# Binding the copies of the weight sums behind the projection's stores, and the residual's scaling into VectorE's operations

## The chip, the cores and the metric

The kernel runs on one core of a Trainium2 chip. A core has TensorE (PE, matrix products; PEld is its loading of weights), VectorE (DVE), ScalarE (ACT) and GpSimd (POOL), each with its own in-order queue of instructions, and 16 DMA engines. Transfers are issued here from two queues: SyncE's (SP), which does nothing else, and POOL's. On each queue a transfer that has to wait for a semaphore holds up everything written behind it. The metric is device time in microseconds (us); lower is better. The profile is one execution, with its own time.

## What is computed

One decoder layer on x of 2048 tokens by 1024 channels (float32), with a conditioning vector c that gives six rows of shift, scale and gate:

```
mod = silu(c) @ w_ada + b_ada            -> sh1, sc1, g1, sh2, sc2, g2
h   = x * (1 + sc1) + sh1
z   = h @ w_in                           -> gate_b, gate_c, v_conv, v_pool (512 columns each)
mix = [gate_b * conv3(gate_c * v_conv), pool(v_pool) @ w_pool * pool_scale] @ w_out
x   = LayerNorm(ALPHA * x + (1 + g1) * mix) * ln1_g + ln1_b        ALPHA = 2 ** 0.25
h   = x * (1 + sc2) + sh2
f   = relu(h @ w_mlp_in) ** 2 @ w_mlp_out                          hidden width 4096
out = LayerNorm(ALPHA * x + (1 + g2) * f) * ln2_g + ln2_b
```

`pool` is a causal mean over windows of 2, 4, 8 and 16 tokens minus the token.

## The kernel before

**Precision.** Every float32 operand is split into a high and a low part (`split`, L81 on ScalarE and L82 on VectorE), and each product is three matmuls (`mm3`, L86 to L88): high by high, high by low, low by high.

**Batches and stages.** The tokens are worked in two batches of T = 1024 (`b` = 0 and 1). Each goes through the input projection (four groups `j` of columns, with convolution and pooling behind each group), the output projection (`out_proj`), the MLP up (`up`, eight groups of 512 hidden columns) and the MLP down (`down`). The projection of batch 0 (`in_proj_0`) begins with `first_group`, which works through the eight slices of the contraction as they land: two rows of `w_ada`, a slice of `w_in` and a tile of x for each, loaded on SP one behind another (`in_turn`, L101), with the matmuls of L403. The other large products, batch 1's projection (`in_proj_1`) among them, use seven products of blocks in place of eight (`seven`); they need sums of blocks of the weights and of the activations, which are made by VectorE or kept in DRAM.

**The weight sums of the change.** Batch 1's `down` takes one part of its work a level further (the "fine" units, matmuls of L1164): blocks of a quarter's width, with sums of quarters of `w2`. These sums are made without any engine: `sum_quarters` (L997, L1000) issues transfers from DRAM to DRAM on POOL's queue. For each of three sets `n` and two halves, step 0 copies four blocks of 512 KB into `wquart` (eight transfers a set), and steps 1, 2 and 3 add onto them with accumulating transfers (four, two and two a set): 48 transfers in all, 24 copies and 24 accumulations. Sets 0 and 1 read weights that are inputs (`w2q`), set 2 reads sums that batch 0's MLP stores (`w2sum`). In the program they are written in batch 1's projection, behind each group `j`, as `SUM_TURNS` has it, and for the last steps in batch 1's `out_proj`:

```
SUM_TURNS = (((0, 0),), ((1, 0), (0, 1)), ((2, 0), (1, 1), (0, 2)), ((2, 1), (1, 2), (0, 3)))   # (set, step) by group
```

**The stores beside them.** Behind each of the groups 0 to 2 of a projection, `store_mixed` (L342, L344) stores the group's outputs and their sums to `msum`, four transfers on POOL; the output projection loads them on SP. The rows of x that `out_proj` adds come by `load_x` (L860) on POOL, into o buffers; VectorE adds the products to them out of PSUM (L877, L884).

**The residual.** `residual(b)` makes ALPHA times the normalised rows: it loads the two rows ln1_g and ln1_b, broadcast over the partitions (`row`, L211, on SP), scales both by ALPHA on ScalarE (L1105, L1106), then for each of eight tiles loads the normalised tile from `nsave` (L1109; on POOL in batch 1, on SP in batch 0), multiplies and adds on VectorE (L91) and stores to `rsave` (L1112). It is a generator: `down` starts it at one unit of its work (`next(later)`), which issues the row loads, and resumes it at four later ones (`later.send(done)`), each of which does two tiles. `done` is the pair of the last instructions of a weight split, ScalarE's and VectorE's.

**The order.** A planner makes the order on each engine's queue: of the instructions whose inputs and buffers its own estimate takes for ready it issues the one that stands first in the program, so an instruction without inputs may come far ahead of its place. `tc.issue_after(i)` orders what its block issues on i's engine behind i, and binds nothing on other engines. Buffers are shared by tag: 28 of `h`, 12 of `o`, 6 of `w`, 5 of `r`, 8 PSUM banks.

Of the kernel before, what the change touches and what calls it, by code (L numbers as in the profile page):

```python
# [11 lines left out]
ALU = mybir.AluOpType  # L12
# [5 lines left out]
H = 512  # L18
# [8 lines left out]
ALPHA = 2.0 ** 0.25  # L27
# [16 lines left out]
def tile_hybrid_layer(ctx: ExitStack, tc: tile.TileContext, opening, xT, x, wada, vec, win0, win,  # L44
                      wins, wpool, wout, wmix, w1, w2, w2q, rows, out):
    nc = tc.nc
# [18 lines left out]
    def t_o(w=T, dt=F32):  # L65
        return mk(big, [P, w], dt, "o", 12)
# [23 lines left out]
    def tt(out_, a, b_, op):  # L90
        return nc.vector.tensor_tensor(out_, a, b_, op=op)  # L91
# [84 lines left out]
    msum = tc.dram_tile([7, NG - 1, P, H], F32, name="msum")  # L176
# [154 lines left out]
    def mixed_sums(y, pt, u, v):  # L331
        a11, a21, a12, a22 = y[:, :H], y[:, H:], pt[:, :H], pt[:, H:]
        s1, s2, s4 = u[:, :H], u[:, H:T], v[:, :H]
        tt(s1, a21, a22, ALU.add)
        tt(s2, s1, a11, ALU.subtract)
        tt(a21, a11, a21, ALU.subtract)
        tt(s4, a12, s2, ALU.subtract)
        return a21, s1, s2, s4

    def store_mixed(j, y, pt, u, v):  # L340
        for i, r in ((0, y), (2, pt), (4, u[:, :T])):
            nc.gpsimd.dma_start(msum[i : i + 2, j].rearrange("a p n -> p a n"),  # L342
                                r.rearrange("p (a n) -> p a n", a=2))
        nc.gpsimd.dma_start(msum[6, j], v[:, :H])  # L344


    def first_group(A):
# [268 lines left out]
    def in_proj_1(X, W, first_w):  # L616
        mixed = []
        ops = Operands(mixed)

        def cut(rows_, h):  # L620
            return [r[:, o + h * H : o + h * H + H] for r, o in rows_]

        def keep(dst, banks):
            for p in range(2):
                nc.scalar.copy(dst[p], banks[p])

        def add(dst, banks):
            for p in range(2):
                tt(dst[p], dst[p], banks[p], ALU.add)

        def group(j):
            x_, y_, z_ = {}, {}, {}
            ready = W if j == 0 else block_weights(wins[j])
            product = seven(ready, X, None if j else first_w)
            v, u = t_o(WW), t_o(WW)
            values = (v, HALO), (u, 2)
            product(0, x_, True)
            keep(cut(values, 0), x_)
            nc.vector.tensor_copy(v[:, :HALO], vhalo[:, j, :])
            nc.vector.tensor_copy(u[:, :2], uhalo[:, j, :])  # L640
            if j == 0:
                inputs(X, ORDER[3][1])
            product(1, y_, True)
            add(cut(values, 0), y_)
            if j == 0:
                inputs(X, ORDER[4][1])
            yield
            gc, gb = t_o(), t_o()
            gates = (gc, 0), (gb, 0)
            last = j == NG - 1  # L650
            product(2, x_, False)
            keep(cut(values, 1), x_)
            if j == 0:
                inputs(X, ORDER[5][1])
            product(3, z_, True)
            keep(cut(gates, 1), z_)
            if j == 0:
                inputs(X, ORDER[6][1])
            if last:
                ops.begin(0)  # L660
            yield
            product(4, x_, False)
            add(cut(gates, 1), x_)
            if last:
                ops.begin(1)
            product(5, z_, False)
            add(cut(values, 1), z_)
            if last:
                ops.weights(0, 1)
                pt = pool_mid(1, j, v)  # L670
            product(6, x_, False)
            keep(cut(gates, 0), x_)
            if last:
                ops.weights(1, 1)
                ops.second(0)
            yield
            if not last:
                pt = pool_mid(1, j, v)
            y = gc
            for hs in halves if last else [slice(0, T)]:  # L680
                w = hs.stop - hs.start
                tt(u[:, 2 + hs.start : 2 + hs.stop], u[:, 2 + hs.start : 2 + hs.stop], gc[:, hs], ALU.mult)
                conv(j, u[:, hs.start : hs.stop + 2], y[:, hs], w)
                tt(y[:, hs], y[:, hs], gb[:, hs], ALU.mult)
                if last and hs.start == 0:
                    mixed.extend([y[:, :H], None, pt[:, :H], pt[:, H:]])
                    ops.third(0)
                    ops.third(1)
            sums = mixed_sums(y, pt, u, v)
            if last:  # L690
                mixed[1] = sums[0]
                mixed.extend(sums[1:])
            else:
                store_mixed(j, y, pt, u, v)
            for n, step in SUM_TURNS[j]:
                sum_quarters(n, step)

        groups = [group(j) for j in range(NG)]
        for _ in range(3):
            next(groups[0])  # L700

        for j in range(1, NG):
            last = j == NG - 1
            next(groups[j])
            if not last:
                next(groups[j])
            next(groups[j - 1], None)
            if last:
                next(groups[j])
            next(groups[j])  # L710
        next(groups[-1], None)
        return ops


    SUM_TURNS = (((0, 0),), ((1, 0), (0, 1)), ((2, 0), (1, 1), (0, 2)), ((2, 1), (1, 2), (0, 3)))
# [276 lines left out]
    def sum_quarters(n, step):  # L992
        for hf in range(2):
            for i, what in SUM_STEPS[step]:
                src = quarter_sum(n, hf, int(what)) if what in ("0", "1") else weight_quarter(n, what, hf)
                if step:
                    nc.gpsimd.dma_start(quarter_sum(n, hf, i), src, accum_op=ALU.add,  # L997
                                        max_dma_last_dim=4096)
                else:
                    nc.gpsimd.dma_start(quarter_sum(n, hf, i), src)  # L1000
# [100 lines left out]
    def residual(b):  # L1101
        ag, ab = row(t_o(D), rows[0]), row(t_o(D), rows[1])
        after = yield
        with tc.issue_after(after[0]):
            nc.scalar.mul(ag, ag, ALPHA)  # L1105
        nc.scalar.mul(ab, ab, ALPHA)  # L1106
        for t in range(8):
            r = t_o(D) if b else t_r()
            (nc.gpsimd if b else nc.sync).dma_start(r, nsave[t])  # L1109
            tt(r, r, ag, ALU.mult)  # L1110
            tt(r, r, ab, ALU.add)
            nc.gpsimd.dma_start(rsave[t], r)  # L1112
            if t % 2:
                yield


    def down(b, F, g2, close):
# [158 lines left out]
        for n, (kind, i, part_) in enumerate(units):  # L1276
            while ahead_ < len(units) and (
                    ahead_ <= n + 1 or b and held + size[units[ahead_][0]] <= 28):
                made.append(operands(*units[ahead_]))
                held += size[units[ahead_][0]]  # L1280
                ahead_ += 1
            ops, done = made.pop(0)
            if made and made[-1][1]:
                done = made[-1][1]
            if kind == "f":
                fine_product(i, part_, ops)
                if (i, part_) == (1, 6):
                    for t in range(4):
                        add(t, lo_, X[t])
                if (i, part_) == (3, 6):  # L1290
                    for t in range(4):
                        tt(F[t][:, hi_], F[t][:, hi_], F[t + 4][:, hi_], ALU.add)
            else:
                if b == 0 and n < 2:
                    ada(G2 + 4 * n, G2 + 4 * n + 4, nc.sync.dma_start, lambda: t_o(D))
                if b == 0 and 2 <= n < 6:
                    sum_x(n - 2, done)
                if n == (0 if b else 5):
                    next(later)
                if kind == "c" and i == 0 and part_ in (1, 2, 4, 6) or b == 0 and 5 <= n < 9:  # L1300
                    later.send(done)
                if kind == "h" and i in (4, 6) and part_ == 1:
                    rest[i] = saved(hi_ if i == 4 else lo_)
                    if i == 6:
                        close.turn()
                banks, new, then = table[i]
                whole = kind == "h"
                matmuls(banks, ops, new, part_ == 0, part_ == (1 if whole else NC - 1), then,
                        part_ == 1 and i in (4, 5, 6) if whole else False)
            held -= size[kind]  # L1310
            if b == 0 and n == 4:
                row_of(g2, mod[:, G2 : G2 + KD])
# [177 lines left out]
```

## Time and profile before

| | |
|---|---|
| median of 3 runs | 1828.07 us (1827.97 to 1833.69) |
| profiled execution, its own time | 1825.45 us |
| its span | 1823.6 us |
| mean granted clock of TensorE | 0.977 |
| TensorE busy | 1741.1 us, 95% |
| VectorE, ScalarE, GpSimd busy | 1329.2, 894.0, 276.2 us |
| moved by DMA | 514.04 MB, 282 GB/s in the mean |

The span runs from the first to the last instruction on the chip; the time of the execution holds a little more. Busy time of TensorE is the sum of overlapping matmuls cut to the clock, so a stretch without a gap reads as wholly busy. The granted clock is the share of full speed that TensorE was given. In the views, "x8" counts instructions, a bracket says how long the engine stood idle before and what released it, "SPq" and "POOLq" are the queues, q1 the transfers of SP and q0 those of POOL.

### The profile page before, as it was taken

The numbers are of one execution on the slowest core, as the hardware profiler recorded it, in microseconds if no ns is written. First come the engines' busy times: TensorE is split into PE (matmuls) and PEld (weight loads), VectorE is DVE, ScalarE is ACT, GpSimd is POOL, SyncE is SP. The second block draws the span as 40 slices with busy tenths as digits, with TensorE's granted clock in tenths as the row PEclk, the third lists the DMA queues.
The fourth block names the chain that finished last, engine by engine and source line by source line (L and its number), as shares of the span: only waits on it lengthen the run. The fifth ranks groups of instructions, "written<-read, shape, count | busy, mean of one in ns | idle before, by whom it ended". The sixth has DMA issues, their size and how long they took to land.

```text
span 1823.6 us, 22633 instructions
## 1 busy us (share of the span) xinstructions
PE 1741.1 (95%) x8132; PEld 1455.6 (80%) x8132; DVE 1329.2 (73%) x1756; ACT 894.0 (49%) x1206; POOL 276.2 (15%) x493
## 2 busy tenths in 40 slices
PE   4599999999988999999999999999999999999998
PEld 3488888888876887888887888888888887999986
DVE  2289869887748649676868778878766667997675
ACT  1242335855434545453557334585545455676552
POOL 3112222112323310000100001011222112000000
PEclk6799999999998999999999999999999999999999
DMA  9999986777898899988876227576455449999884
GB/s 316 269 384 354 349 312 219 283 265 294 334 289 331 325 337 417 390 298 301 321 284 231 88 99 280 173 250 222 169 211 205 168 176 380 419 407 325 309 311 182
DMA packets 158304, 514.04 MB, mean 282 GB/s; under 512 B 18288, under 2 KB 23920, under 8 KB 157936
## 3 DMA queue, kind: packets, MB, share of 16 engines
q1 hardware_dynamic: 102960, 315.97, 47.5%
q0 software_dynamic: 55232, 196.64, 30.4%
q8 instruction: 63, 1.03, 0.2%
q14 instruction: 49, 0.40, 0.1%
HBM read 359.97 MB, written 177.73 MB: 295 GB/s over the span
## 4 chain that ended last, share of the span: by engine, by line
PE 79%; DMA 12%; DVE 3%; issue 3%; ACT 2%; POOL 1%; SPq 0%; DVEq 0%; POOLq 0%; ACTq 0%
PE ps L87 24%; PE ps L88 24%; PE ps L86 24%; PE ps L1164 7%; DMA o<-in_xT 5%; DMA r<-usum 2%; DVE o L91 1%; PE ps L403 1%; DMA wquart<-w2sum 1%; PE ps L758 1%; DMA w<-in_w 1%; DVE h L82 1%; DMA usum<-o 1%; DMA winsum<-o 1%; DMA r<-in_xT 0%
## 5 line engine op out<-in xcount | busy, mean ns | idle before, releaser
L88 PE MATMUL ps<-h,w 128*128 128x512 f32 x1312 | 511.2, 390 | 10.8 <-DVE w L82 10.8
L86 PE MATMUL ps<-h,w 128*128 128x512 f32 x1312 | 510.9, 390 | 5.6 <-ACT o L1014 4.5
L87 PE MATMUL ps<-h,w 128*128 128x512 f32 x1312 | 510.8, 390 | 0.0
L87 PE MATMUL ps<-h,h 128*128 128x512 f32 x928 | 362.3, 391 | 3.5 <-DVE h L82 3.5
L88 PE MATMUL ps<-h,h 128*128 128x512 f32 x928 | 362.0, 390 | 0.0
L86 PE MATMUL ps<-h,h 128*128 128x512 f32 x928 | 361.8, 391 | 0.1
L81 ACT CAST h<-r 128x1024 fp32r<-128x1024 f32 (+1 forms) x202 | 205.5, 1021 | 244.4 <-PE ps L87 105.6
L82 DVE TENSOR_TENSOR h<-r,h 128x1024 fp32r<-128x1024 f32 (+1 forms) x202 | 238.2, 1184 | 94.3 <-ACT h L81 92.1
L88 PEld LDWEIGHTS ps<-h,w 128*128 128x128 f32 x1312 | 246.7, 188 | 63.0 <-DVE w L82 12.3
L81 ACT CAST w<-r 128x1024 fp32r<-128x1024 f32 x156 | 164.4, 1054 | 265.7 <-PE ps L87 256.8
L86 PEld LDWEIGHTS ps<-h,w 128*128 128x128 f32 x1312 | 246.4, 188 | 58.7 <-ACT o L1014 5.4
L87 PEld LDWEIGHTS ps<-h,w 128*128 128x128 f32 x1312 | 246.6, 188 | 51.9 <-DVE h L82 0.5
L82 DVE TENSOR_TENSOR w<-r,w 128x1024 fp32r<-128x1024 f32 x156 | 190.6, 1222 | 119.0 <-ACT w L81 117.5
L91 DVE TENSOR_TENSOR o<-o,o 128x1024 f32<-128x1024 f32 (+2 forms) x238 | 202.5, 862 | 48.8 <-DMA usum<-o 40.7
L87 PEld LDWEIGHTS ps<-h,h 128*128 128x128 f32 x928 | 174.8, 188 | 40.2 <-DVE h L82 4.2
L86 PEld LDWEIGHTS ps<-h,h 128*128 128x128 f32 x928 | 174.8, 188 | 36.5 <-ACT h L81 0.5
L88 PEld LDWEIGHTS ps<-h,h 128*128 128x128 f32 x928 | 174.7, 188 | 36.3
L82 DVE TENSOR_TENSOR h<-w,h 128x1024 fp32r<-128x1024 f32 x114 | 139.0, 1219 | 15.4 <-ACT h L81 15.4
L91 DVE TENSOR_TENSOR o<-o,ps 128x512 f32<-128x512 f32 (+1 forms) x168 | 110.1, 664 | 52.8 <-PE ps L88 52.6
L81 ACT CAST h<-w 128x1024 fp32r<-128x1024 f32 x114 | 119.7, 1050 | 24.4 <-DMA w<-in_w 14.5
L1164 PE MATMUL ps<-h,h 128*128 128x256 f32 x1008 | 126.1, 286 | 4.5 <-ACT h L81 3.5
L1164 PEld LDWEIGHTS ps<-h,h 128*128 128x128 f32 x1008 | 125.0, 195 | 6.3 <-ACT h L81 3.7
(157 smaller groups left out, 1445.9 us busy)
## 6 DMA issues: line engine op xcount, KB each, us to landing
usum<-o POOLq DMA_DIRECT2D x88, 512.0 KB, 4.2
r<-usum SPq DMA_DIRECT2D x88, 512.0 KB, 6.5
w<-w2sum SPq DMA_DIRECT2D x62, 512.0 KB, 7.7
r<-in_w SPq DMA_DIRECT2D x60, 512.0 KB, 5.7
r<-uquart SPq DMA_DIRECT2D x42, 512.0 KB, 7.6
o<-in_w SPq DMA_DIRECT2D x72, 256.0 KB, 6.2
w2sum<-o POOLq DMA_DIRECT2D x64, 256.0 KB, 5.6
w<-in_w SPq DMA_DIRECT2D x32, 512.0 KB, 8.2
```

The source lines that it names most:

```text
L81: high = nc.scalar.copy(hi, src)
L82: return high.ins, nc.vector.tensor_tensor(lo, src, hi.bitcast(F32), op=ALU.subtract).ins
L86: nc.tensor.matmul(ps, whi, xhi, start=first, stop=False, skip_group_check=goes_on)
L87: nc.tensor.matmul(ps, whi, xlo, start=False, stop=False, skip_group_check=goes_on)
L88: nc.tensor.matmul(ps, wlo, xhi, start=False, stop=last, skip_group_check=goes_on)
L91: return nc.vector.tensor_tensor(out_, a, b_, op=op)
L403: nc.tensor.matmul(ps[m, h], wt[:, w : w + P], A[k][p // 2][:, hs], start=k == 0 and p == 0, stop=k == KD - 1 and p == 2)
L758: nc.tensor.transpose(ps[:, t * P : t * P + P], R[4 * h + t][:, k * P : k * P + P], ident)
L1164: nc.tensor.matmul(ps, a[:, us], w[:, gs], start=not begun, stop=hf == 1 and g == 3 and a is ul, skip_group_check=True)
```

## The change

`store_mixed` returns its last store. In batch 1's projection the steps of `sum_quarters` behind groups 0, 1 and 2 are ordered behind that group's last store on POOL; those behind the last group stay free. In `residual` the two ScalarE scalings go; VectorE's multiply and add become three-operand instructions that multiply by ALPHA as well; the first of them is ordered behind VectorE's half of a weight split. In batch 1 the residual starts at unit 2 in place of 0, and its four turns come at the groups 3, 4, 5, 6 of the first product in place of 1, 2, 4, 6.

```diff
     def store_mixed(j, y, pt, u, v):
...
-        nc.gpsimd.dma_start(msum[6, j], v[:, :H])
+        return nc.gpsimd.dma_start(msum[6, j], v[:, :H]).ins
...
             else:
-                store_mixed(j, y, pt, u, v)
-            for n, step in SUM_TURNS[j]:
-                sum_quarters(n, step)
+                done = store_mixed(j, y, pt, u, v)
+            with nullcontext() if last else tc.issue_after(done):
+                for n, step in SUM_TURNS[j]:
+                    sum_quarters(n, step)
...
         after = yield
-        with tc.issue_after(after[0]):
-            nc.scalar.mul(ag, ag, ALPHA)
-        nc.scalar.mul(ab, ab, ALPHA)
         for t in range(8):
             r = t_o(D) if b else t_r()
             (nc.gpsimd if b else nc.sync).dma_start(r, nsave[t])
-            tt(r, r, ag, ALU.mult)
-            tt(r, r, ab, ALU.add)
+            with tc.issue_after(after[1]):
+                nc.vector.scalar_tensor_tensor(r, r, ALPHA, ag, op0=ALU.mult, op1=ALU.mult)
+            nc.vector.scalar_tensor_tensor(r, ab, ALPHA, r, op0=ALU.mult, op1=ALU.add)
...
-                if n == (0 if b else 5):
+                if n == (2 if b else 5):
                     next(later)
-                if kind == "c" and i == 0 and part_ in (1, 2, 4, 6) or b == 0 and 5 <= n < 9:
+                if kind == "c" and i == 0 and part_ in (3, 4, 5, 6) or b == 0 and 5 <= n < 9:
                     later.send(done)
```

## The prediction

> **What bounds the kernel now.** I read the totals of the page, then TensorE's busy time in stretches of 45 us, to see where it does not run.
>
> ```profile
> span 1823.6 us, 22633 instructions
> PE 1741.1 (95%) x8132; PEld 1455.6 (80%) x8132; DVE 1329.2 (73%) x1756; ACT 894.0 (49%) x1206; POOL 276.2 (15%) x493
> ```
>
> ```profile
> 0.00:45.00 45.00, 17.73 (x70) 14.26 (x71) 10.02 (x28) 6.89 (x11) 16.71 (x50) 0.67 0.96 316
> 45.00:90.00 45.00, 23.58 (x75) 18.00 (x75) 13.57 (x24) 11.62 (x17) 5.73 (x7) 0.73 1.06 269
> ...
> 495.00:540.00 45.00, 41.45 (x183) 34.03 (x182) 26.68 (x31) 18.44 (x22) 15.23 (x24) 1.00 1.02 303
> 540.00:585.00 45.00, 35.56 (x151) 28.99 (x150) 29.30 (x34) 18.41 (x22) 11.66 (x22) 0.89 0.88 315
> ...
> 675.00:720.00 45.00, 42.28 (x180) 34.54 (x179) 32.64 (x39) 24.16 (x26) 0.54 (x1) 0.96 1.03 415
> ...
> 1035.00:1080.00 45.00, 45.00 (x201) 37.24 (x200) 33.73 (x39) 13.97 (x18) 4.77 (x7) 1.00 0.32 114
> 1080.00:1125.00 45.00, 45.00 (x200) 37.28 (x199) 36.62 (x39) 21.42 (x26) 4.36 (x7) 1.00 0.65 232
> ...
> 1530.00:1575.00 45.00, 40.49 (x246) 36.73 (x245) 40.74 (x37) 27.24 (x32) 3.74 (x7) 0.92 1.03 417
> ```
>
> The columns are the stretch, its length, then busy time (and count) of PE, PEld, DVE, ACT and POOL, the granted clock, the DMA share and GB/s. TensorE is 95% busy, and a full stretch holds 200 of the large matmuls (1080:1125), 0.225 us each. So time is to be had only where this row falls short: the first 90 us (41.3 busy), 495 to 585, 675 to 720, and 1530. In all of them the DMA share is 0.88 or more. Who holds the DMA engines? The view by queue for the first 90 us, and the view of the tile that the copies write:
>
> ```profile
> q0 software_dynamic: 2741, 16.54, 70.9%
> q1 hardware_dynamic: 3166, 9.76, 30.0%
> ```
>
> ```profile
> L1000 POOL DMA_DIRECT2D wquart<-in_w2q x16: 488/488/635, 1.8 to 20.3; - x16
> L997 POOL DMA_DIRECT2D wquart<-wquart x12: 814/819/849, 38.1 to 668.4; - x12
> L997 POOL DMA_DIRECT2D wquart<-in_w2q x8: 805/814/881, 21.8 to 34.1; - x8
> L1000 POOL DMA_DIRECT2D wquart<-w2sum x8: 706/820/1057, 502.4 to 634.1; - x8
> L997 POOL DMA_DIRECT2D wquart<-w2sum x4: 1176/1196/1227, 516.1 to 648.1; - x4
> ```
>
> The columns of the first are packets, MB and share of the 16 engines; of the second, min/median/max ns of issue and first to last start. The weight sums are written in the second batch's projection, but the planner put them wherever their inputs allowed: 32 of the 48 transfers at the head of the program, the other 16 at 502 and 632 us. POOL's queue (q0) takes 70.9% of 90 us = 63.8 us of all engines for 16.54 MB, about 32 transfers of 0.52 MB: **2.0 us of all 16 engines each**. SP's loads (q1), which feed the first projection group, get 30%. The chain of waits says that these loads set the start:
>
> ```profile
> 4.59 38.65 DMA o<-in_xT
> ...
> 96.75 16.66 PE ps L403 x72
> ```
>
> TensorE ends the first group at 96.75 + 16.66 = 113.4 us.
>
> **Part 1, the start.** Binding the copies that begin the sums to a store in the second batch's projection takes all 32 transfers from here: the accumulating steps need the copies' results and follow them. What is late next is the larger of SP's own loads and TensorE. Loads: vecs 0.04 MB, opening 3 x 0.52, half an xT tile 0.26, then seven times 2 x 0.52 + 0.26 + 0.52; 14.7 MB. In the stretch from 100 to 125 us q1 runs nearly alone:
>
> ```profile
> DMA packets 3152, 10.32 MB, mean 413 GB/s; under 512 B 350, under 2 KB 606, under 8 KB 3150
> ...
> q1 hardware_dynamic: 2891, 9.32, 92.1%
> ```
>
> At 413 GB/s the loads take 36 us, and one of the seven steps 4.4 us. TensorE's step is 16.66 / 3 = 5.55 us, so TensorE sets the pace: eight steps, 44.4 us. It can begin when the opening (1.8 MB, 4.4 us after the first 2 us) is in and its modulation and split are made, about 10 us. End 54.4; for the clock I add 2 us. **113.4 - 56.4 = 57 us saved.** From below: if short gaps hold the whole group at the 0.67 that the first stretch was granted, the eight steps take 44.4 / 0.67 = 66 us and the gain is 37; from above, without the 2 us and with a start at 9, 60.
>
> The clock needs the row first: the two stretches at the start were granted 0.67 and 0.73, and TensorE was busy in about half of their time. The Trainium skill (TensorE: Matmul & The Clock Gate, Part 1) says that the array is at half clock by default and that about 3.4 us of sustained work release it; by that rule the penalty would be one or two such windows, 2 to 3 us. That hangs on TensorE running without long gaps here, which no run shows yet.
>
> **Part 2, the first batch's MLP.** POOL runs its queue in order, and an accumulation waits there for the copy before it:
>
> ```profile
> 502.44 2.95 POOL L1000 DMA_DIRECT2D wquart<-w2sum  x4 [0.25 <-issue]
> ...
> 536.88 0.85 POOL L997 DMA_DIRECT2D wquart<-wquart  x1 [7.83 <-DMA wquart<-wquart]
> 537.43 2.45 POOL L1030 DMA_DIRECT2D usum<-o  x4
> ```
>
> Behind it wait the stores of the hidden blocks (usum), behind these the o buffers, then ScalarE's copies out of PSUM, then TensorE. The two stretches from 495 hold 183 + 151 matmuls for 400: 66 x 0.225 = **15 us saved**, clock loss included. The same happens at 632, where the last usum stores, and with them the loads of the down-projection, are late: 180 of 200 at 675, 4.5 us; the DMA share stays high there with SP's own loads (415 GB/s), so I take **4**. Together 19, between 12 and 21.
>
> **Part 3, where the 48 transfers go.** 8 copies behind the stores of group 0, 12 transfers behind group 1's, 14 behind group 2's, 8 unbound ones of group 3 that depend on these, 6 later. The program's stores and what stands behind them on POOL:
>
> ```profile
> 1037.59 0.57 POOL L344 DMA_DIRECT2D msum<-o  x1
> ...
> 1103.76 0.57 POOL L344 DMA_DIRECT2D msum<-o  x1
> 1109.05 0.55 POOL L860 DMA_DIRECT2D o<-in_x  x1 [4.72 <-PE ps L87]
> ...
> 1127.30 0.53 POOL L860 DMA_DIRECT2D o<-in_x  x1 [14.27 <-issue]
> ```
>
> ```profile
> o<-in_x POOLq DMA_DIRECT2D x16, 512.0 KB, 6.6
> ```
>
> ```profile
> 1141.70 2.48 DVE L877 SCALAR_TENSOR_TENSOR o<-o,ps 128x512 f32<-128x512 f32 x4
> ```
>
> The first 20 fall into stretches at a DMA share of 0.32 and 0.65 and cost 40 engine-us in 66; I take 2 us for slower weight loads (0 to 6). From 1104 the 22 next (14 + 8) are ready for the planner before the residual rows x (L860) have a free buffer, and are written before them; so the rows, above all the fourth (1127 now), stand behind 22 x 2.0 = 44 us of engine time. VectorE takes the rows at 1141.7 to 1144.2 to empty the PSUM banks, on which TensorE's third product waits. At the 0.7 share of the first 90 us the rows come at 1104 + 63 + 6.6 (a row's own landing) = 1174, alone on the engines at 1104 + 44 + 6.6 = 1155: 11 to 30 us late. A stalled TensorE stops SP's loads too, so the truth lies between; I take **20 us lost**. Bounds: 0, if the rows get ahead; 45, if the operands' loads on SP, at 30% of the engines, are late besides.
>
> A rule speaks against the change as well: the Trainium skill (DMA: Bandwidth & Descriptors, Queues, rings and completion order) has each engine take turns between queues by packet. The trace agrees, with 2741 packets of q0 beside 3166 of q1 in the first 90 us; so SP's loads have no precedence over sums that only the second batch's down-projection reads.
>
> **Part 4, the residual.** Two ScalarE scalings a batch go:
>
> ```profile
> L1106 ACT ACTIVATE o<-o x2: 1057/1060/1062, 762.1 to 1536.8; 128x1024 f32<-128x1024 f32 x2
> ```
>
> ```profile
> L91 DVE TENSOR_TENSOR r<-r,o 128x1024 f32<-128x1024 f32 x16 | 19.2, 1221 | 16.9 <-DMA r<-nsave 16.8
> ...
> L1366 DVE SCALAR_TENSOR_TENSOR o<-o,mv,w 128x1024 f32<-128x1024 f32 (+1 forms) x17 | 20.6, 1218 | 1.5 <-ACT mv L723 1.1
> ```
>
> 4 x 1.06 us, on an engine that is 49% busy: nothing, except that the last (1536.8) stands in ScalarE's queue ahead of casts for the fine products; that is in the gap costed below. On VectorE three-operand instructions of the same shape take 1.22 us like the two-operand ones, 32 before and 32 after: nothing. In the second batch two row loads on SP and up to five reloads on POOL leave the place where TensorE stops:
>
> ```profile
> 1526.59 2.72 POOL L1109 DMA_DIRECT2D o<-nsave  x5
> ```
>
> 7 x 0.52 MB at 417 GB/s are 8.8 us of DMA in front of what the first fine product needs. TensorE's gap there is 45 - 40.49 = 4.5 us, plus a few at half clock; I take **3 us saved**, between 0 and 7. Against it: the scalings on VectorE are now bound behind a weight split, and the splits behind them in VectorE's queue wait for a late reload; in the first batch VectorE lost 16.8 us so with TensorE covered by operands loaded ahead. At the narrower place that cover may be gone: up to 6 us, taken as nothing.
>
> **The sum.** 1823.6 - 57 - 19 + 2 + 20 - 3 = 1766.6. The profiled execution's own time is 1825.45, 1.85 above its span, and the median of the runs 1828.07, 2.6 above that: 1766.6 + 1.85 + 2.6, about **1771 us**.
>
> **The rivals.**
> (a) No backlog at the output projection: the residual rows get ahead, or the sums are done sooner than at the start, where they shared with a full SP queue. Against it stands the fourth row's late buffer. 1771 - 20 - 2 = 1749.
> (b) The backlog is heavier, 45 us: SP's loads are late too. For it: the stretch from 1080 is at 0.65 already. 1796.
> (c) The start keeps a low clock: 37 saved in place of 57, 1791. Against it: with gap-free work the clock is 1.00, as from 1080 on.
> (d) The change doesn't do what it says, since the planner finds another early place: 1828. The bound is an order on POOL behind a store that needs the second batch's results; little speaks for it.
> (e) Slower. The accumulations run one after another as POOL's worst stretch shows:
>
> ```profile
> 38.10 0.81 POOL L997 DMA_DIRECT2D wquart<-wquart  x1 [3.21 <-DMA wquart<-in_w2q]
> 45.63 0.81 POOL L997 DMA_DIRECT2D wquart<-wquart  x1 [6.71 <-DMA wquart<-in_w2q]
> ```
>
> 7.5 us each; the 14 accumulations of the 22 take 105 us, the 8 copies 16, so the rows come at 1104 + 121 + 6 = 1231, 87 late: 1771 + 67 = 1838. It decides from 6.8 us an accumulation on, where the loss passes 77 us.
>
> **How the numbers follow.** Forecast 0.45, (a) 0.25, (b) 0.13, (c) 0.10, (d) 0.02, (e) 0.05. I count 0.3% (5.5 us) as what a measurement of this kernel tells from no change. Faster is the first four, 0.93; within 0.3% is (d), 0.02; slower (e), 0.05. The forecast's own range, from the bounds of parts 1 to 4, is 1758 to 1788; the range down to (a) with its upper gain and up past (b) and (c) is 1742 to 1802.
>
> **What would show it.** Right: the copies (wquart) first start after 1037 less the time saved; the first group ends near 56; 200 matmuls in every stretch of the first batch's MLP; a gap of TensorE at the second output projection with VectorE waiting for the rows of x. Wrong: a first group that ends past 70; copies before 900; or an output projection without a gap (then (a)). It would be wrong altogether if TensorE loses more than 77 us there.

## The result, and the profile after

The changed kernel takes 1802.17 us (median of 4 runs, 1800.89 to 1806.26) against 1828.03 for the kernel before: ratio 0.9855, 95% interval 0.9830 to 0.9879. That is faster by 26 us where 57 were forecast, a hair above the range's upper end. The profiled execution took 1806.26 us, the longest of the four, and its span is 1804.5; the stage times below are those of profiled executions.

The same stretches as before, in the view of TensorE's busy time (same columns), with those of the second projection added:

```profile
0.00:45.00 45.00, 42.08 (x192) 35.34 (x193) 35.85 (x78) 25.78 (x38) 2.07 (x26) 0.96 0.97 385
45.00:90.00 45.00, 45.00 (x204) 37.37 (x203) 39.45 (x68) 15.55 (x23) 10.43 (x18) 1.00 0.86 324
...
495.00:540.00 45.00, 45.00 (x200) 37.29 (x199) 34.45 (x40) 23.45 (x27) 10.75 (x20) 1.00 0.81 307
540.00:585.00 45.00, 45.00 (x201) 37.26 (x200) 33.58 (x38) 27.02 (x33) 11.19 (x21) 1.00 0.86 318
...
990.00:1035.00 45.00, 41.52 (x177) 33.72 (x176) 34.34 (x38) 14.85 (x19) 12.44 (x20) 0.97 0.81 244
1035.00:1080.00 45.00, 36.48 (x141) 28.42 (x141) 27.62 (x33) 14.59 (x21) 14.79 (x18) 0.88 1.02 292
1080.00:1125.00 45.00, 15.49 (x63) 12.38 (x62) 12.39 (x22) 5.72 (x6) 12.21 (x17) 0.70 1.02 244
1125.00:1170.00 45.00, 41.70 (x191) 34.42 (x190) 30.60 (x61) 26.29 (x53) 4.90 (x8) 0.96 0.71 226
```

The gaps at the start and in the first batch's MLP are gone. A new one, larger than forecast, has opened between 990 and 1170: 572 matmuls where a full TensorE does 800, so 228 x 0.225 = 51 us.

To see where each microsecond went, I read the start of one instruction that ends each stage, in every trace, and took differences. "Start" is TensorE's last matmul of the first group (L403), "batch 0" from there to the row of g2 in its down-projection (the weight load of L142), "projection" from the first to the last bank that ScalarE keeps in the second batch's in_proj_1 (L625), "output projection" from there to VectorE's last accumulation (L884 before, L885 after), "MLP" from there to the last bank kept (L1014, L1015), "products" from there to the last fine matmul. Two more columns, from g2's row to the projection (205 to 208 us) and the tail (102 to 104), are much the same everywhere.

| us | start | batch 0 | projection | output projection | MLP | products |
|---|---|---|---|---|---|---|
| before | 113.0 | 656.2 | 154.5 | 73.0 | 292.7 | 225.9 |
| after | 54.9 | 635.2 | 172.8 | 110.2 | 292.5 | 228.0 |
| difference | -58.1 | -21.0 | +18.3 | +37.2 | -0.2 | +2.1 |

The two early gains, 79 us, are nearly those of the forecast (57 and 19). Of these, 55.5 us are given back in the second batch's projection and its output projection, where the forecast had 22. The mechanism it named is there. POOL's queue, in order of time (start, us, what; the bracket is the idle time before and what ended it):

```profile
961.77 2.95 POOL L1001 DMA_DIRECT2D wquart<-in_w2q  x6
...
1001.09 2.94 POOL L1001 DMA_DIRECT2D wquart<-in_w2q  x6
...
1034.80 0.59 POOL L344 DMA_DIRECT2D msum<-o  x1
1035.39 3.72 POOL L1001 DMA_DIRECT2D wquart<-w2sum  x5
...
1078.03 1.15 POOL L998 DMA_DIRECT2D wquart<-w2sum  x1 [8.73 <-issue]
1093.70 1.17 POOL L998 DMA_DIRECT2D wquart<-w2sum  x1 [14.53 <-issue]
1094.33 3.95 POOL L998 DMA_DIRECT2D wquart<-wquart  x4
1096.92 3.00 POOL L861 DMA_DIRECT2D o<-in_x  x3
```

From 1035.39 on, 22 transfers stand ahead of the rows of x (L861), and they keep the queue for 61.5 us. The chain of waits of the same execution gives the row's own landing, VectorE's queue the length of the wait, and the waits of TensorE from 900 to 1180 (total, times, longest) what it cost:

```profile
1096.92 16.61 DMA o<-in_x
```

```profile
1113.66 0.69 DVE L878 SCALAR_TENSOR_TENSOR o<-o,ps 128x512 f32<-128x512 f32 x1 [30.73 <-DMA o<-in_x]
```

```profile
PE ps L86 <- DVE o L878: 30.7, 2, 29.5
PE ps L86 <- DVE o L91: 8.5, 3, 3.3
```

So far as forecast: the rows are late and VectorE waits for them with the PSUM banks full. Not forecast is what ScalarE's queue shows earlier, still in the projection:

```profile
1024.50 1.05 ACT L81 CAST h<-r 128x1024 fp32r<-128x1024 f32 x1 [11.27 <-DMA r<-msum]
...
1047.40 1.04 ACT L81 CAST h<-r 128x1024 fp32r<-128x1024 f32 x1 [7.15 <-DMA r<-gout]
...
1059.14 1.04 ACT L81 CAST h<-r 128x1024 fp32r<-128x1024 f32 x1 [5.12 <-DMA r<-msum]
```

These casts prepare the output projection's operands. They wait for loads on SP, and ScalarE works in order, so the projection's own evictions of PSUM stand behind them. From 985 to 1180 such casts waited 35.0 us for msum in all and 48.3 for gout; in the same part of the kernel before it was 9.1 and 12.5, no wait longer than 5.6. Who holds the engines? The view by queue from 1010 to 1035 (packets, MB, share of the 16 engines):

```profile
q0 software_dynamic: 864, 4.72, 73.7%
q1 hardware_dynamic: 874, 2.28, 27.0%
```

In this stretch both queues get the same number of packets, but one of q0's lasts 0.737 x 25 x 16 / 864 = 0.34 us and one of q1's 0.12, so equal turns leave SP a quarter of the engines. The Trainium skill (DMA: Bandwidth & Descriptors, Queues, rings and completion order) says that each DMA engine takes turns between its queues by whole packets; the 864 beside 874 agree. The next two stretches of 25 us agree less closely, with 1353 beside 1042 and 1373 beside 1066; SP's shares there are 32.3% and 30.0%.

### The profile page after: what moved, and what is told of

Read it like the earlier page. It is cut to its first block, busy times and chain, and to the rows that moved or that the text cites. A ratio compares the mean times of both kernels' runs of the same rounds, so it can differ in the third digit from the quotient of the medians.

```text
span 1804.5 us, 22616 instructions
## 1 busy us (share of the span) xinstructions
PE 1735.6 (96%) x8132; PEld 1452.8 (81%) x8132; DVE 1330.3 (74%) x1756; ACT 890.4 (49%) x1202; POOL 276.5 (15%) x493
## 3 DMA queue, kind: packets, MB, share of 16 engines
q0 software_dynamic: 55232, 196.64, 30.6%
q8 instruction: 63, 1.03, 0.2%
## 4 chain that ended last, share of the span: by engine, by line
PE 80%; DMA 8%; DVE 5%; issue 4%; ACT 2%; POOL 1%; SPq 0%; DVEq 0%; POOLq 0%; ACTq 0%
PE ps L87 24%; PE ps L86 24%; PE ps L88 23%; PE ps L1163 6%; PE ps L403 3%; DMA wquart<-in_w2q 2%; DVE h L82 1%; DVE o L91 1%; DMA o<-in_x 1%; PE ps L759 1%; DMA r<-msum 1%; DMA r<-in_xT 1%; DVE o L1365 1%; DVE o L1359 1%; ACT h L81 0%
## 5 line engine op out<-in xcount | busy, mean ns | idle before, releaser
L86 PE MATMUL ps<-h,h 128*128 128x512 f32 x928 | 364.0, 393 | 36.6 <-DVE o L878 30.7
L91 DVE TENSOR_TENSOR o<-o,o 128x1024 f32<-128x1024 f32 (+2 forms) x222 | 183.3, 836 | 24.1 <-DMA usum<-o 17.8
L91 DVE TENSOR_TENSOR o<-o,ps 128x512 f32<-128x512 f32 (+1 forms) x168 | 110.2, 663 | 54.4 <-PE ps L88 54.0
```

What stands on the lines that cost most here:

```text
L86: nc.tensor.matmul(ps, whi, xhi, start=first, stop=False, skip_group_check=goes_on)
```

## The experiments

Theory A: what costs is the order in POOL's queue, with the rows of x behind the sums. Theory B: the sums keep the DMA engines from SP's operand loads. A third question is what a transfer costs, and a fourth what the residual's edit does. Ratios are against the kernel before, with 95% intervals.

**The floor: no sums at all.** The calls in the projection and those in the output projection go.

```diff
-            with nullcontext() if last else tc.issue_after(done):
-                for n, step in SUM_TURNS[j]:
-                    sum_quarters(n, step)
...
-                    nc.sync.dma_start(q, wquart[n, hf, int(w) - 1])
+                    nc.sync.dma_start(q, w2q[n % 2, int(w) - 1, hf])
```

> The changed kernel with all 48 transfers left out; the fine products read quarters of the input in place of the sums, so the result isn't the reference's, while every load, split and matmul stays. It gives the floor: the time with no sums anywhere. By the ledger: 1828 less 58 (start) less 21 (first batch's MLP) plus 2.8 (residual) = 1751 to 1752, if the 55 us of the second projection are all due to the sums. If something else in the edit lost them, it stays near 1802. The distance to the kernel with the sums in the second batch's MLP (1760) is then what the 48 transfers still cost there: 8.

Measured: 1748.56 us (1747.1 to 1750.03), 0.9564 (0.9551 to 0.9577). The projection takes 153.9 and the output projection 73.7 us, as before the change (154.5 and 73.0). So all of the 55.5 us come from the sums. The page's row by queue, of this kernel and then of the changed one, gives their price:

```profile
q0 software_dynamic: 48576, 171.47, 25.6%
```

```profile
q0 software_dynamic: 55232, 196.64, 30.6%
```

0.306 x 1804.5 - 0.256 x 1748.3 = 104.6 us of all 16 engines for 48 transfers, 2.2 each. The forecast's 2.0 was nearly right as a mean.

**What adding costs.** The 24 accumulating transfers become plain copies of the same pieces.

```diff
                 if step:
-                    nc.gpsimd.dma_start(quarter_sum(n, hf, i), src, accum_op=ALU.add,
-                                        max_dma_last_dim=4096)
+                    nc.gpsimd.dma_start(quarter_sum(n, hf, i), src, max_dma_last_dim=4096)
```

> The changed kernel with its 24 accumulating transfers made plain copies of the same pieces (no addition, so the fine products read quarters that aren't summed); number, bytes, order and binding are as in the changed kernel. It measures what adding costs. The forecast took 2.0 us of all engines for every transfer. From the run without sums, 48 cost 104.6 us (30.6% of 1804.5 less 25.6% of 1748.3), and 8 copies 12.6 us in the stretch from 945, 1.6 each, which leaves 2.8 for an accumulation. If so, 24 x 1.2 = 29 us of engine time go, 17 of them ahead of the rows: 1802 - 20 to 30 = 1772 to 1782. If the piece size is what costs and not the addition: 1798 to 1804.

Measured: 1779.23 us (1777.31 to 1783.59), 0.9730 (0.9711 to 0.9749). The row by queue:

```profile
q0 software_dynamic: 53696, 196.64, 29.3%
```

0.293 x 1777.7 = 520.9 us against 552.2 of the changed kernel: 31.3 us over 24, so adding costs 1.3 us; a copy costs (520.9 - 447.6) / 48 = 1.5, an accumulation 2.8. The 22 transfers ahead of the rows hold 14 accumulations: 8 x 1.5 + 14 x 2.8 = 51 us of engines, not the forecast's 44. With copies alone the loss in the two stages falls from 55.5 to 32.1 (projection 169.3, output projection 90.3). The edit takes out packets too (55232 to 53696), so the price of adding holds for these transfers with their pieces.

**Fewer transfers there, and the two early gains apart.** First only sets 0 and 1 are bound (the edit against the changed kernel), then only set 2 (against the run just above it).

```diff
-            with nullcontext() if last else tc.issue_after(done):
-                for n, step in SUM_TURNS[j]:
+            for n, step in SUM_TURNS[j]:
+                with nullcontext() if last or n == 2 else tc.issue_after(done):
                     sum_quarters(n, step)
```

> The changed kernel, but the sums of set 2 (those that read the first batch's sums of blocks) are unbound as before; sets 0 and 1 stay bound, so 8 copies stand behind group 0, 12 transfers behind group 1 and 11 in place of 22 before the rows of x. The start keeps its 58 us, the first batch's MLP has its 21 us of stall back. If the loss in the second projection follows the engine time that the sums take there (11 accumulations x 2.8 = 31 us in place of some 55 to 60), the rows come some 25 to 30 us earlier and the loss of 55 falls to 20 to 30: 1802 + 21 - 30 = 1793 (1786 to 1798). If any backlog at this place costs about the same, since operands and rows come late one after the other: 1815 to 1823.

Measured: 1791.88 us (1789.43 to 1794.24), 0.9795 (0.9780 to 0.9809). The start takes 52.6, batch 0 658.3 us: the start's gain is kept, the MLP's is gone. Projection and output projection take 173.8 and 73.5, a loss of 19.8. The time is as expected, the place of the loss is not: 19.3 of the 19.8 lie in the projection, and though 11 transfers stand ahead of the rows of x, TensorE doesn't wait for the rows at all. The chain of waits goes by operand loads on SP:

```profile
1031.03 14.35 DMA r<-msum
...
1062.93 21.02 DMA r<-wosum
```

```diff
-                with nullcontext() if last or n == 2 else tc.issue_after(done):
+                with nullcontext() if last or n < 2 else tc.issue_after(done):
```

> The complement: only set 2's sums are bound, sets 0 and 1 go out at the start as before. The start's 58 us are not gained, the first batch's MLP gives its 21 us. In the second projection nothing is added behind groups 0 and 1, and 12 transfers (8 copies, 4 accumulations; about 24 us of engine time) stand before the rows. By engine time there is room for them (the DMA share without sums is 0.73 and 0.51 in the two stretches from 1035, 34 us free): loss under 10, 1828 - 21 + 5 = 1812 (1808 to 1817). If a dozen transfers ahead of the rows is enough to stall: 1822 to 1830.

Measured: 1826.86 us (1825.14 to 1829.78), 0.9988 (0.9979 to 0.9998). Start 113.1, batch 0 635.1: the MLP's 21 us are there, and they belong to set 2 alone. But 20.2 of them are lost again (projection 165.1, output projection 82.6), though 12 transfers should have fitted into the free engine time. My expectation fell. Free time in a stretch of 45 us is no cover when the transfers go out in one burst, as POOL's queue has it here:

```profile
1085.32 4.48 POOL L1001 DMA_DIRECT2D wquart<-w2sum  x6
...
1121.26 1.15 POOL L998 DMA_DIRECT2D wquart<-w2sum  x1 [6.57 <-issue]
1121.88 3.22 POOL L861 DMA_DIRECT2D o<-in_x  x5
```

The 12 transfers hold the queue for 36.5 us, 3 us each, where by the prices above they need 8 x 1.5 + 4 x 2.8 = 23 us of engines to themselves; the DMA share of the stretch from 1080 is 1.03.

**The rows first.** The 22 transfers are bound behind the fourth row of x, then behind the eighth; then set 2's 12 transfers, alone bound, behind the eighth.

```diff
-            with nullcontext() if last else tc.issue_after(done):
+            if j < 2:
+              with tc.issue_after(done):
                 for n, step in SUM_TURNS[j]:
                     sum_quarters(n, step)
...
         for _ in range(4):
-            load_x()
+            row_ = load_x()
+        if b:
+            with tc.issue_after(row_):
+                for n, step in SUM_TURNS[2] + SUM_TURNS[3]:
+                    sum_quarters(n, step)
```

> The changed kernel, but the sums of groups 2 and 3 (the 22 transfers) are bound behind the load of the fourth row of x instead of behind group 2's stores; so the rows go first, and the same bytes then move during the same output projection. Theory A, the order in POOL's queue is what costs: VectorE's wait of 30.7 us for the rows goes, the output projection loses under 10 us in place of 37.2, about 1770 (1765 to 1777). Theory B, what costs is that the sums hold some 70% of the DMA engines while SP's operand loads are wanted: TensorE then waits for operands where it waited for rows, the loss stays above 25 us, 1790 to 1802. Third way: the rows of the second half (5 to 8) now stand behind the sums, and the wait only moves to matmuls(3), 1780 to 1790.

Measured: 1795.83 us (1792.07 to 1797.03), 0.9811 (0.9795 to 0.9827). The projection's loss falls from 18.3 to 6.8 us, the output projection's stays (38.8 against 37.2): TensorE now waits once, 24.7 us, for VectorE and a row of the second half (rows 5 to 8), which stands behind the 22. That is the third way, at theory B's time; it doesn't part A from B.

> As the kernel with the first four rows of x ahead of the 22 transfers, but they are bound behind the eighth row, so no row of x stands behind a sum. With four rows ahead, VectorE waited once for 24.7 us for a row of the second half, which stood behind the 22. Theory A (order in POOL's queue): that wait goes too, 1796 - 20 to 25 = 1770 to 1776. Theory B (shared DMA engines): operands on SP come late in its place, 1790 to 1800. Third way: the normalised rows' stores (nsave) and the transposed blocks' (hsave) now stand behind the sums, and the loads of the MLP's operands wait for them: 1780 to 1790.

Measured: 1796.53 us (1794.2 to 1798.38), 0.9826 (0.9813 to 0.9839). No row stands behind a sum now, and nothing is gained by it: the projection loses 6.5, the output projection 40.2. The waits of TensorE from 900 to 1260, and its stretches:

```profile
PE ps L86 <- DVE o L880: 14.5, 3, 6.8
PE ps L86 <- ACT w L81: 12.8, 1, 12.8
```

```profile
1080.00:1125.00 45.00, 30.53 (x108) 23.82 (x107) 19.67 (x31) 15.55 (x25) 11.45 (x13) 0.81 1.04 255
1125.00:1170.00 45.00, 32.10 (x151) 25.93 (x150) 19.11 (x47) 22.40 (x54) 8.76 (x14) 0.86 1.00 265
```

The one long wait has become several: operands late on SP (theory B; the DMA share is at 1.04 and 1.00), and then a weight of the MLP, 12.8 us late, since its buffer is freed by a store that now stands behind the sums. The chain of waits has that store and the load behind it:

```profile
1148.17 13.16 DMA hsave<-r
...
1161.39 4.92 DMA r<-in_w
```

Theory A as I had put it is wrong: putting the rows first moves the wait, it doesn't remove it. But the wait that it moves to stands in POOL's queue again, since the store of hsave comes behind the sums. So these two runs don't say how much of the loss would stay if nothing at all stood behind the 22.

```diff
-            with nullcontext() if last else tc.issue_after(done):
-                for n, step in SUM_TURNS[j]:
+            for n, step in SUM_TURNS[j]:
+                if n < 2:
                     sum_quarters(n, step)
...
+            row_ = load_x()
+        if b:
+            with tc.issue_after(row_):
+                sum_quarters(2, 0)
+                sum_quarters(2, 1)
```

> As the kernel with set 2's sums alone bound, but its 12 transfers stand behind the eighth row of x in place of group 2's stores. There the 12 took 36.5 us of POOL's queue (1085.3 to 1121.9), the rows landed 14.6 us after their issue in place of 6.6, and projection and output projection together took 247.7 us in place of the 227.5 before. If with so light a load the order in the queue is what costs, the rows are in time and the loss falls from 20 to 6 or less: 1826.9 - 14 to 20 = 1807 to 1813. If it is what the sums take from SP's operand loads while they run, or the stores that now stand behind them: 1820 to 1828.

Measured: 1819.72 us (1818.38 to 1820.68), 0.9947 (0.9928 to 0.9965), between the two expectations. The loss is 12.7 us (projection 153.8, output projection 86.4) against 20.2 with the same 12 transfers ahead of the rows. So with a light load the order costs some 7.5 us, and 12.7 remain with the rows ahead. The chain of waits names operands' loads on SP in their place, the longest of them:

```profile
1129.80 16.81 DMA r<-msum
```

In the kernel before, such a load lands in 5.8 us in the median, by the view of DMA issues (KB each, median us to landing):

```profile
r<-msum SPq DMA_DIRECT2D x14, 512.0 KB, 5.8
```

**Another place.** All 48 transfers go out in the second batch's MLP, each step bound behind the last store of one of its groups; the calls in the projection and the output projection go.

```diff
-    SUM_TURNS = (((0, 0),), ((1, 0), (0, 1)), ((2, 0), (1, 1), (0, 2)), ((2, 1), (1, 2), (0, 3)))
+    SUM_TURNS = (((0, 0),), ((1, 0),), ((2, 0),), ((0, 1), (1, 1)), ((2, 1), (0, 2)), ((1, 2), (2, 2), (0, 3)),
+                 ((1, 3), (2, 3)), ())
...
-        save(c11, 7)
+        done = save(c11, 7)
+        if fine:
+            with tc.issue_after(done):
+                for n, step in SUM_TURNS[g]:
+                    sum_quarters(n, step)
```

> The changed kernel, but all 48 transfers go out in the second batch's MLP, each step bound behind the last store of one of its groups 0 to 6 (8, 8, 8, 8, 6, 6, 4 transfers), a group apart from the copies they add to. The MLP's DMA share there is 0.44 to 0.58 with TensorE full, so 40% of 260 us = 104 us of all engines are free for 48 x 2.0 to 2.8 = 96 to 134 us. If both the queue and the shared engines cost time only where TensorE has no slack: the 55 us lost in the second projection come back, 1802 - 55 = 1747. Rival: accumulations hold POOL's queue as they did in the first batch's MLP (15 us lost to 16 transfers), the stores of the hidden blocks come late, and up to 48/16 x 15 = 45 us are lost there: 1755 to 1790. It decides whether a place with free engines is enough.

Measured: 1759.9 us (1759.36 to 1760.98), 0.9619 (0.9605 to 0.9633). Projection and output projection are back at 152.8 and 74.8; the MLP takes 304.4 in place of the 292.9 without sums, 11.5 lost. Its two broken stretches, and the piece of the chain of waits in the first of them:

```profile
1215.00:1260.00 45.00, 40.82 (x170) 33.29 (x169) 26.65 (x35) 20.62 (x25) 14.41 (x25) 0.92 0.70 245
...
1395.00:1440.00 45.00, 40.64 (x173) 33.22 (x172) 25.38 (x34) 22.08 (x27) 12.36 (x18) 0.96 0.92 274
```

```profile
1220.04 15.21 DMA r<-in_w
```

A weight takes 15.2 us to land right after two bursts of 8 copies (the changed kernel's median for these loads is 5.7). The next kernel puts 8 copies behind group 0 of the projection and spreads the other 40, with the residual as before.

```diff
+    SUM_TURNS = (((1, 0),), ((0, 1),), ((2, 0),), ((1, 1), (0, 2)), ((2, 1), (0, 3)), ((1, 2), (2, 2)),
+                 ((1, 3), (2, 3)), ())
...
                 done = store_mixed(j, y, pt, u, v)
+            if j == 0:
+                with tc.issue_after(done):
+                    sum_quarters(0, 0)
```

> As the sums in the second batch's MLP with the residual as before, but 8 copies go out behind group 0's stores in the projection, where the DMA share is 0.29 and TensorE is full, and the other 40 in the MLP as 8, 4, 8, 6, 6, 4, 4 by groups, so that no two bursts of 8 follow one another. With the two bursts, TensorE lost 4.2 us in the stretch from 1215 (a weight load of 15 us) and 4.4 us in that from 1395. If bursts are what still costs: 4 to 8 us less than without the spreading, 1749 to 1753. If it is the total of bytes in the MLP: 1755 to 1757.

Measured: 1748.4 us (1748.13 to 1752.05), 0.9573 (0.9560 to 0.9586): the time of the kernel without sums (1748.56), which has the new residual. The edit changes two things at once, the spreading and the number in the MLP (40 for 48), so it doesn't part them. From 945 to 1440 no stretch of 45 us loses more than 1.3; two of them:

```profile
1215.00:1260.00 45.00, 45.00 (x200) 37.26 (x199) 29.84 (x41) 22.97 (x28) 18.86 (x27) 1.00 0.81 243
...
1305.00:1350.00 45.00, 45.00 (x201) 37.24 (x200) 32.14 (x41) 22.72 (x26) 15.39 (x20) 1.00 1.04 259
```

TensorE is full in the stretch with a DMA share of 1.04, about the share at which it stood still in the output projection. This version beats both kernels, by 79.5 us and by 54.

**The residual.** Its edit alone on the kernel before (`residual` and the two conditions in `down`, as in the change's diff), then the sums' binding alone, then the MLP version with the residual as before.

> The kernel before with the residual's edit alone (scaling inside VectorE's two operations, two units later); the sums' copies stay where they were. The prediction's part 4 (the row loads leave the place where TensorE stops, 3 us gained): 1825. The ledger of the two traces (2.8 us lost between the last MLP group and the end, since the loads still go out beside the second batch's last hidden blocks and only VectorE's operations moved, into the fine units): 1831. No effect: 1828.

Measured: 1830.94 us (1826.22 to 1835.58), 1.0006 (0.9996 to 1.0017), so between 0.7 us faster and 3.1 slower; a gain of 3 is excluded. The products take 227.7 us against 225.9.

> The changed kernel with the residual as before, so only the weight sums are bound. By the ledger (residual costs 2.8 us): 1799. By the prediction's part 4 (residual gains 3 us): 1805. If the two edits meet nowhere, this run's gain and that of the residual alone add up to the whole change's.

Measured: 1798.88 us (1797.76 to 1801.07), 0.9829 (0.9815 to 0.9843), as the ledger had it; the interval overlaps that of the whole change (0.9830 to 0.9879), so the 3.3 us between them are not clear of the noise.

> The kernel with all sums in the second batch's MLP, and the residual as before. If the residual's edit costs the same 3.3 us here as it did beside the bound sums (1798.9 against 1802.2): 1759.9 - 3.3 = 1756.6. If that difference was an accident of the order that the planner found there (alone, on the kernel before, the edit moved nothing: ratio 1.0006): 1760.

Measured: 1759.39 us (1758.14 to 1764.49), 0.9629 (0.9615 to 0.9642); with the new residual it was 1759.9, so in the whole time the residual's edit shows no difference here. The products are 2.5 us shorter (226.7 against 229.2), but the MLP is 2.5 longer (306.9 against 304.4). Over all traces the products take 225.9 to 227.5 us with the old residual (4 kernels) and 227.7 to 229.6 with the new (10 kernels): the new one costs some 2 us there, at the edge of what the times can show. The loads did not move: POOL's queue of the changed kernel has them beside the last group's stores, 22 us earlier in the program's time like all else (1526.59 before).

```profile
1504.07 2.14 POOL L1107 DMA_DIRECT2D o<-nsave  x4
```

Only VectorE's operations are bound by the edit, and the planner takes a load as soon as a buffer is free. VectorE now does them between 1534 and 1571, four at a time, amid the fine products, whose splits keep it wholly busy (45.00 of 45 us from 1530). Before, they stood there too, from 1537 to 1591. In the changed kernel TensorE waits for it there, which it didn't in the kernel before:

```profile
PE ps L1163 <- ACT h L81: 3.7, 1, 3.7
PE ps L1163 <- DVE o L91: 2.4, 1, 2.4
```

The first row is the gap that the edit was to shorten: 3.5 us before, 3.7 after. That the 2.4 us are the cost is argued from this trace; other kernels with the new residual lose the 2 us in other waits.

## Why the prediction was wrong

**Part 1, right.** 57 forecast, 58.1 measured. TensorE's first group sets the pace as worked out: its last matmul starts at 54.9, the end was put at 56.4. The two us for the clock were spent in this execution, by the stretches of the changed kernel's first 30 us (0.83 is the granted clock of the second):

```profile
0.00:10.00 10.00, 7.08 (x45) 6.62 (x46) 4.57 (x19) 3.02 (x5) 1.39 (x25) 1.00 0.78 270
10.00:20.00 10.00, 10.00 (x37) 8.04 (x38) 9.21 (x18) 5.68 (x10) 0.00 (x0) 0.83 1.03 418
20.00:30.00 10.00, 10.00 (x46) 8.26 (x44) 8.82 (x17) 6.82 (x11) 0.00 (x0) 1.00 1.03 415
```

17% of 10 us are 1.7. In stretches of 2 us the clock falls to 0.84, 0.50 and 0.81 between 10 and 16, after TensorE had stood still for 1.86 us. The rule that I had set beside it, of some 3.4 us at half clock until the array is released (the Trainium skill, TensorE: Matmul & The Clock Gate, Part 1), gives, as an estimate, the same 1.7 for one such stay, and the low clock of the start, rival (c), did not last. But the two us are not a fixed cost of this start. The nine other kernels that begin without the copies were granted 1.00 in the same stretch, and their first group's last matmul starts at 52.6 to 53.6, so 59 to 60 us are saved. The kernel with the sums alone bound, for one:

```profile
10.00:20.00 10.00, 9.99 (x44) 7.79 (x43) 9.37 (x18) 5.68 (x10) 0.00 (x0) 1.00 1.03 417
```

**Part 2, right.** 19 forecast, 21.0 measured, and the run that binds set 2 alone has these 21 us without the start's gain.

**Part 3, right in the mechanism, wrong in its two sizes; this is the step that failed.** The backlog at the output projection was put at 20 (0 to 45) and measured 37.2. The 22 transfers were counted rightly, and the 63 us that they would need at a share of 0.7 came out (61.5), in part by luck: by the prices above the 22 need 51 us of all engines and not 44, and POOL's share was 67 to 91%. I then took a value between that and the 44 us of engines to themselves, on the ground that a stalled TensorE stops SP's loads. That is the step of the working that failed. TensorE stands still for long only from 1083 on, and SP's share falls only then, from 32% and 30% in the stretches from 1035 and 1060 to 7.9% from 1085, when the rows are already late. So the trace took the long end: VectorE waited 30.7 us, the top of the 11 to 30 worked out. Two things that the sum didn't have lengthened it: the accumulations cost 2.8 us of engines (as plain copies, 23 of the 55.5 us go), and the row itself landed in 16.6 us in place of 6.6, with five accumulations issued just ahead of it. The slower loads of the projection, put at 2 (0 to 6), measured 18.3, outside their bounds. I had costed the 20 transfers behind groups 0 and 1 by averages of the DMA share and had asked only for weights. The output projection's operands are loaded in the same stretch, ScalarE casts them in order ahead of the evictions, and SP got a quarter of the engines. With the 22 moved behind the rows 6.5 to 6.8 of the 18.3 remain, so some 12 of them are the 22 transfers' too. Rival (b), heavier because SP's loads are late too, had the mechanism right, at 45 us and a chance of 0.13; the two stages together lost 55.5.

That the order in the queue is the cause, as the working had it, is shown for part of the loss only. With the rows first the two stages get back 9 to 10 us of 55.5 (the whole kernel 6), with the lighter load 7.5 of 20.2. What remains with the lighter load, and the whole 19.8 with sets 0 and 1 alone, goes by operand loads on SP. With all 22 the split stays open, since something else of POOL's queue comes to stand behind them, and taking one wait away lengthens the next. That the place decides is shown by the MLP: all 48 cost it 14.0 us there, and 40 of them spread out cost it 1.2 (residual as before, against the 292.9 without sums).

**Part 4, wrong in sign, small.** 3 us of gain forecast (0 to 7), about 2 lost in the products, at the edge of the noise; a gain of 3 is excluded. The premise that the row loads leave the place was wrong: only the VectorE operations are bound. What I had named against it and taken as nothing, scalings in VectorE's queue at a place without cover, is the nearer account, but argued from one trace.

The sum with the measured terms: 1823.6 - 58.1 - 21.0 + 18.3 + 37.2 + 2.1, and 2.4 for what isn't named (from g2's row on 1.9, the tail 0.7, the MLP -0.2), gives the span of 1804.5. Of the 37.9 us by which the forecast span of 1766.6 was short, the two terms of part 3 make 33.5. The range from 1742 to 1802 was narrower than its own terms: with all the bounds given in parts 1 to 4 at once, the sum reaches from 1740 to 1830, and the forecast's own range of 1758 to 1788 can't be had from them. The range took one rival at a time, and here two terms were off together.

## What to carry to other kernels

A transfer that nobody needs soon is still not free to place: put it where the stage's own loads have slack ahead of their use (here the MLP), spread out, not where TensorE's next operands are loaded just in time; the mean DMA share of a stretch doesn't tell these apart. Price accumulating DMAs apart from copies, at about twice a copy here. And before costing a wait by the queue order alone, ask what ends next if the order is mended: here a second wait, 24.7 us for 30.7, stood behind it.

## What the runs showed of the hardware

An accumulating transfer of 0.52 MB between places in DRAM took 2.8 us of all 16 DMA engines in the mean and the copy 1.5. In the stretch from 1010 to 1035 two queues moved 864 and 874 packets, and POOL's longer packets held 74% of the engines' time. And 40 transfers in the MLP cost it 1.2 us (294.1 against 292.9 without sums) at a DMA share of up to 1.04, while 12 in one burst cost 20 us in the projection and output projection, whose DMA shares without sums were 0.73 and 0.51 in the two stretches of 45 us from 1035.
